# Token operands of the stationary side laid out in turns, read with a step of two elements

## The chip, the cores and the metric

The kernel runs on one core of one Trainium2 chip. The metric is the device time of one launch in microseconds. The profile shows TensorE as two rows: PE for the matmuls and PEld for the loads of their stationary operand.

## What is computed

The reference is an encoder trunk of two layers over 256 tokens of width 2048. Cut to its frame, one layer is:

```python
h = rms_norm(x, ln1_g[l])
proj = h @ w_in[l]                       # 2048 -> 4608 columns: q, k, v of two head groups
...                                      # QK norm, rotary, two kinds of windowed attention -> oa, ob
o = jnp.concatenate([rms_norm(oa, on_a[l]), rms_norm(ob, on_b[l])], axis=-1)
x = x + o @ w_out[l]                     # 2048 -> 2048
h2 = rms_norm(x, ln2_g[l])
u = depthwise_conv(h2 @ w_up[l], conv_w[l], conv_b[l])   # 2048 -> 2 x 5632, three taps over tokens
gate, up = u[..., :D_FF], u[..., D_FF:]
x = x + (jax.nn.silu(gate) * up) @ w_down[l]             # 5632 -> 2048
```

Everything is float32.

## The kernel before

**Numbers.** Every float32 operand of a large product is split in two float32r parts, a high one (ScalarE copies it with rounding) and a low one (VectorE subtracts the high part from the original). A product is then three matmuls: high by high, low by high and high by low. A tile of split tokens has the shape 128 x 2 x 256: partitions hold 128 of the features, then come the two parts, then the 256 tokens.

**Which side is stationary.** In the input projection (`q_win`), the output projection (`q_wout`), and the down-projection (`q_seven`, `q_plain`, `q_down`) 128 tokens are the stationary operand (a tile of 128 x 128) and 512 columns of weights move. In the up-projection (`q_up`) it is the other way: 128 columns of weights are stationary, and the tokens move, 512 columns for both parts or 256 for the high part alone. `q_seven` computes most of the down-projection by Strassen-like products: it takes sums and differences of token halves (`sums_mid`), which are split as the tokens are, and of weight blocks (`sums_first`, `sums_second`).

**The two halves.** The 256 tokens are two halves of 128, since a stationary operand has 128 columns. Before the change, half 0 stands in elements 0 to 127 of a part and half 1 in 128 to 255, so a stationary operand is 128 elements in a row. The tile names that the profile uses: `xs` are the split tokens of the two norms, `mid` (and, where the feed-forward needs more of them, `qT` and `qtok`) the split outputs of attention `os`, of the gate `gs` and of the sums `ss`; `whi` and `wlo` are the high and low parts of weights (some of them in `kT`, `v_a` and `v_b`). In a matmul's row the moving tile stands first after the arrow and the stationary one second: `mm<-whi,xs` has weights moving over stationary tokens, `mm<-xs,whi` tokens moving over stationary weights.

**Where the split tokens are written.** `prep_x` writes `xs` (argument `which` is 0 for the norm ahead of the input projection, 1 for the one ahead of the up-projection), `values` writes `os`, `high` and `low` in `glu` write `gs` out of `ms`, and `high` and `low` in `sums_mid` write the sums. Each of these is one instruction of 256 elements on ScalarE for the high part and one on VectorE for the low part. `ms`, the sums in `tq` and the PSUM tiles that they read keep their order of tokens.

**Order of work.** Weights come by DMA in tiles of 128 x 1024 (`raw`), in the order of a list of quanta, and are split some steps ahead of their matmuls (`split_w`, `high_w`, `low_w_dve`); part of the low parts are made by a DMA that adds (`low_w`). From the second of the feed-forward's 44 column blocks on, a class `Plan` sets the order on PE, ScalarE, VectorE and GpSimd by a table of due times and durations; elsewhere the framework's scheduler does. Some tile sizes are padded (1024 + 64 elements, `UP_AT`, `SHIFT`) so that tiles start at chosen addresses.

Of the kernel before, what the change touches and what calls it, by code (L numbers as in the profile page):

```python
# [11 lines left out]
F32 = mybir.dt.float32  # L12
F32R = mybir.dt.float32r
I32 = mybir.dt.int32
AF = mybir.ActivationFunctionType
# [3 lines left out]
P = 128  # L19
L = 2  # L20
T = 256
# [105 lines left out]
def encoder_kernel(  # L127
# [5 lines left out]
    nc = tc.nc  # L133
# [19 lines left out]
    ln_g = head[:, 0:2 * L * KD].rearrange("p (w l k) -> p w l k", w=2, l=L)  # L153
# [10 lines left out]
    def mm(ps, lhsT, rhs, start, stop):  # L164
        nc.tensor.matmul(ps, lhsT, rhs, start=start, stop=stop, skip_group_check=True)  # L165

    def rsqrt(ps, inv_n, dst, tag):
# [5 lines left out]
            e = e.rearrange("p (t h) -> p t h", t=TT)  # L173
        nc.gpsimd.tensor_tensor(dst, v, e, op=ALU.pow)

    def split(hi, lo, src, scale=None):

        if scale is None:
            high = nc.scalar.activation(hi, src, AF.Copy)  # L179
            nc.vector.tensor_sub(lo, src, hi.bitcast(F32))  # L180
        else:
            high = nc.scalar.activation(hi, src, AF.Copy, scale=scale)  # L182
            nc.vector.scalar_tensor_tensor(lo, src, scale, hi.bitcast(F32),
                                           op0=ALU.mult, op1=ALU.subtract)
        return high
# [11 lines left out]
    xs = {}  # L197
    st = {}

    def prep_x(l, which, k, src):  # L200

        xs[k] = act.tile([P, 2, T], F32R, name=f"xs{k}")
        split(xs[k][:, 0], xs[k][:, 1], src, ln_g[:, which, l, k:k + 1])

    def square_x(nb):
        if nb == 0:
# [117 lines left out]
    os = {}  # L324
# [147 lines left out]
    def values(l, grp, h):  # L472
        t = sm.pop(("T", grp, h))
        ps = psum.tile([P, T], F32, name="pv", bufs=1)
        if grp == "a":
            v, c = V["a", h // 4], (h % 4) * HD
            mm(ps[:, 0:KW], v[:, 0, c:c + HD], t[:, 0, 0:KW], True, False)
            mm(ps[:, T - KW:T], v[:, 1, c:c + HD], t[:, 1, 0:KW], False, True)
        else:
            v, c = V["b", 0], (h // 4) * HD  # L480
            for kt in range(TT):
                thrice(ps, [v[:, i, kt, c:c + HD] for i in range(2)], [w[:, kt, :] for w in t], kt == 0, kt == TT - 1)
        g = 0 if grp == "a" else 1
        if h == 0:
            acc_o[grp] = act.tile([P, T], F32, name=f"acc_{grp}")
        k = g * NH + h
        os[k] = act.tile([P, 2, T], F32R, name="mid", bufs=MIDS)
        split(os[k][:, 0], os[k][:, 1], ps, par["on_g"][:, l, g, h:h + 1])
        add_square(acc_o[grp], ps, h == 0)


# [11 lines left out]
    def three(ps, terms, hv, lv, first, last, apart=False):  # L503

        n = len(terms)
        order = [(x_part, w, tt) for x_part, w in ((0, hv), (1, hv), (0, lv)) for tt in range(TT)]
        if apart:
            order.sort(key=lambda o: o[2])
        for x_part, w, tt in order:
            for i, x2 in enumerate(terms):  # L510
                mm(ps[:, tt], x2[:, x_part, tt * P:(tt + 1) * P], w[:, i],
                   first and w is hv and x_part == 0 and i == 0, last and w is lv and i == n - 1)

    cur = {}
# [89 lines left out]
    gs = {}  # L604
# [35 lines left out]
    def glu(l, f, q, ps):  # L640
        ux = halo[f % 2]
        r = T // GRID_W
        e = ends.get((l, f), 0.0)
        own = {}
        taps = [[par["conv"][:, l, i, j * NF + f:j * NF + f + 1] for i in range(4)] for j in range(2)]
        k = lambda n, g=f: (n, l, g)

        def read(part):
            own[part] = work.tile([P, 2, T], F32, name="prob", bufs=2)
            with tc.high_priority(offset=4 * AHEAD_PRIO):  # L650
                nc.scalar.activation(own[part], ps[:, :, part], AF.Copy)  # L651

        def scale():
            nc.vector.tensor_mul(ux[:, :, r:r + T], own[0], st["r2"][:, None, :].to_broadcast([P, 2, T]))

        def sides():
            nc.scalar.activation(ux[:, :, 1:r], ux[:, :, T:T + r - 1], AF.Copy)
            nc.scalar.activation(ux[:, :, T + r:T + 2 * r - 1], ux[:, :, r + 1:2 * r], AF.Copy)

        def tap(name, j, o, i):  # L660
            if name not in own:
                own[name] = work.tile([P, 2, T], F32, name="pT", bufs=4)
            src = ux[:, j, o:o + T]
            if name == "y":
                nc.scalar.activation(own["y"][:, j], src, AF.Identity, scale=taps[j][i], bias=taps[j][3])  # L665
            else:
                nc.scalar.activation(own[name][:, j], src, AF.Copy, scale=taps[j][i])  # L667

        def gate():
            m = ms[f] = work.tile([P, T], F32, name="bias", bufs=2)  # L670
            nc.vector.tensor_mul(m, own[0][:, 0, :], own["y"][:, 1, :])

        def high():
            gs[f] = middle(l, f)
            nc.scalar.activation(gs[f][:, 0], ms[f], AF.Copy)

        def low():
            nc.vector.tensor_sub(gs[f][:, 1], ms[f], gs[f][:, 0].bitcast(F32))

        plan.act(k("t"), 512, e + 2.5, lambda: read(0), [("pe", q, 1), k("gate", f - 1)])  # L680
        plan.act(k("t2"), 512, e + 3.0, lambda: read(1), [k("t"), k("sum", f - 1)])
        plan.dve(k("sum"), 512, e + 5.0, lambda: nc.vector.tensor_add(own[0], own[0], own[1]), [k("t"), k("t2")])
        plan.dve(k("scale"), 512, e + 6.0, scale, [k("sum")] + [k(n + str(j), f - 2) for n in "yab" for j in range(2)])
        plan.op(k("sides"), "ACT", 0.3, e + 7.0, sides, [k("scale")])
        for n, o, i, dep, old in (("y", r, 1, "scale", k("add_b", f - 1)), ("a", 0, 0, "sides", k("gate", f - 1)),
                                  ("b", 2 * r, 2, "sides", k("add_a", f - 1))):
            for j in range(2):
                plan.act(k(n + str(j)), T, e + 7.5 + i % 3 + 0.5 * j, lambda n=n, j=j, o=o, i=i: tap(n, j, o, i),
                         [k(dep), old], 2 if n == "y" else 1)
        for n in "ab":  # L690
            plan.dve(k("add_" + n), 512, e + (11.0 if n == "a" else 12.0),
                     lambda n=n: nc.vector.tensor_add(own["y"], own["y"], own[n]),  # L692
                     [k("y0"), k("y1"), k(n + "0"), k(n + "1")])
        plan.act(k("silu"), T, e + 13.0, lambda: nc.scalar.activation(own[0][:, 0, :], own["y"][:, 0, :], AF.Silu),
                 [k("add_a"), k("add_b")])
        old = [("vsum", l, f // 2 - 1), k("low", f - 2)]
        plan.dve(k("gate"), T, e + 14.0, gate, [k("silu")] + old)
        plan.act(k("high"), T, e + 18.0, high, [k("gate")], when=lambda: sum(free.values()) > 0)
        plan.dve(k("low"), T, e + 24.0, low, [k("high")])
        if f % 2 and f < NF - CHUNKS[-1] + PART:  # L700
            sums_mid(l, f // 2)
# [3 lines left out]
    def sums_mid(l, p):  # L705
# [11 lines left out]
            nc.vector.tensor_sub(v[:, 2], m1[:, a], m1[:, b])  # L717
            nc.vector.tensor_sub(v[:, 3], m2[:, a], v[:, 1])

        part = lambda i: own["v"][:, 2 * i:2 * i + 2].rearrange("p j n -> p (j n)")  # L720

        def high(i):
            own[i] = middle(l, 2 * p)
            nc.scalar.activation(own[i][:, 0], part(i), AF.Copy)

        def low(i):
            t = own[i]
            nc.vector.tensor_sub(t[:, 1], part(i), t[:, 0].bitcast(F32))
            for j in range(2):
                ss[p, 2 * i + j] = t[:, :, j * P:(j + 1) * P]  # L730

        reads = [("low", l, 2 * p), ("low", l, 2 * p + 1)]
        plan.dve(k("vsum"), P, e + 24.0, sums, reads + [("vlow1", l, p - 2)], 4)
# [5 lines left out]
    def q_seven(l, c, m, i):  # L739

        f = sum(CHUNKS[:c]) + 2 * i
        p = f // 2
        a, b = slice(0, P), slice(P, T)

        def body(q, part, hi, lo):
            if i == 0 and part == 0:
                t = psum.tile([P, 2, 512], F32, name="mm", bufs=2)
                ps = {1: t[:, 0], 6: t[:, 1]}
                for n, name, k in ((5, "S", 2), (7, "S", 2), (3, "tr", 1), (4, "pv", 1)):
# [1 line left out]
                cur["seven"] = ps  # L751
            ps = cur["seven"]
            hv, lv = (w.rearrange("p (k n) -> p k n", k=2) for w in (hi, lo))
            todo = (((1, gs[f][:, :, a], 1), (3, ss[p, 3], 0)),
                    ((7, ss[p, 2], 0), (5, ss[p, 0], 1)),
                    ((4, gs[f + 1][:, :, b], 0), (6, ss[p, 1], 1)))[part]
            for n, x2, j in todo:
                for x_part, w in ((0, hv), (1, hv), (0, lv)):
                    mm(ps[n], x2[:, x_part], w[:, j], i == 0 and x_part == 0 and w is hv,
# [65 lines left out]
    def q_plain(l, c, m):  # L825

        f0 = sum(CHUNKS[:c])

        def body(q, half, hi, lo):
            ps = cur["seven"][1]  # L830
            hv, lv = (w.rearrange("p (k n) -> p k n", k=2) for w in (hi, lo))
            for x_part, w in ((0, hv), (1, hv), (0, lv)):
                for i in range(2):
                    mm(ps, gs[f0 + 4 * half + 2 * i + 1][:, x_part, 0:P], w[:, i],
                       False, half == 1 and i == 1 and w is lv)
            if half == 1 and m == 1:
                for i in range(PAIRS):
                    drop(l, f0 // 2 + i, (1,))
        return body
# [495 lines left out]
```

## Time and profile before

| | |
|---|---|
| time, median of 3 runs | 2070.07 us (2069.88 to 2070.23) |
| the profiled execution's own time | 2070.64 us |
| its span | 2068.9 us |
| PE busy | 2062.4 us, 10720 matmuls |
| PEld busy | 1769.9 us, 10720 loads |
| VectorE (DVE) busy | 1706.1 us |
| ScalarE (ACT) busy | 1549.3 us |
| GpSimd (POOL) busy | 157.6 us |
| HBM | 412.80 MB read, 201 GB/s over the span |

The span runs from the first to the last instruction on the core. The end of a matmul is modelled in the profile and reaches into the next one, so that the time of a stream of matmuls is read from one start to the next. Stretches, from the start of the span: input projection, attention and output projection up to about 339 us (second layer: from about 1020 to 1369 us), and the feed-forward after each.

### The profile page before, as it was taken

The page shows a single profiled execution, that of the slowest core. Times are in us where ns is not written, and L with a number is a line of the kernel's source. Part 1 is how long each engine was busy: PE and PEld are TensorE (multiplying, and loading weights), DVE is VectorE, ACT ScalarE, POOL GpSimd, SP SyncE. Part 2 cuts the span into 40 slices and gives each one's busy share as a digit, 9 for nine tenths or more (in the row PEclk, how much of TensorE's full clock was granted, in tenths as well). Part 3 has the DMA queues.
Part 4 walks back from the last instruction along what each step waited for, and adds up shares of the span by engine and source line. Part 5 has one row for each costly group of instructions (what it writes and reads, how often), then busy time and mean ns, then how long its engine had stood idle before and what let it go on. Part 6 is the DMA issues. An engine that isn't in the chain of part 4 may idle for free.

```text
span 2068.9 us, 30510 instructions
## 1 busy us (share of the span) xinstructions
PE 2062.4 (100%) x10720; PEld 1769.9 (86%) x10720; DVE 1706.1 (82%) x2576; ACT 1549.3 (75%) x2595; POOL 157.6 (8%) x170
## 2 busy tenths in 40 slices
PE   9999999999999999999999999999999999999999
PEld 8888888888888888888888888888888888888887
DVE  7786655889999999999757866558899999999995
ACT  7566646988888888888555665479888888888883
POOL 0011000000000000000000111000000000000000
PEclk9999999999999999999999999999999999999999
DMA  9655557888888888898655555678788888888883
GB/s 350 204 163 163 171 180 200 256 233 249 256 265 251 257 251 259 250 263 255 219 181 177 173 166 164 191 211 242 239 251 258 254 256 264 256 252 259 253 261 131
DMA packets 134009, 472.48 MB, mean 228 GB/s; under 512 B 15328, under 2 KB 17888, under 8 KB 133856
## 3 DMA queue, kind: packets, MB, share of 16 engines
q1 hardware_dynamic: 117872, 413.87, 61.2%
q0 software_dynamic: 15264, 55.58, 15.0%
q8 instruction: 84, 1.38, 0.3%
q10 hardware_dynamic: 720, 1.08, 0.2%
q14 instruction: 69, 0.57, 0.1%
HBM read 412.80 MB, written 2.10 MB: 201 GB/s over the span
## 4 chain that ended last, share of the span: by engine, by line
PE 99%; DMA 0%; ACT 0%; ACTq 0%; DVE 0%; issue 0%
PE mm L165 85%; PE S L165 6%; PE pv L165 4%; PE tr L165 3%; PE tr L460 1%; PE tr L381 1%; PE S L220 1%; DMA mid<-in_xT 0%; ACT v_a L335 0%; ACT whi L1002 0%; ACT mid L182 0%; ACT xs L182 0%; DVE x L872 0%; ACTq L1105 0%; ACTq L1098 0%
## 5 line engine op out<-in xcount | busy, mean ns | idle before, releaser
L165 PE MATMUL mm<-xs,whi 128*128 128x512 f32 x2320 | 810.0, 390 | 0.0
L1011 DVE TENSOR_TENSOR wlo<-raw,whi 128x1024 fp32r<-128x1024 f32 x503 | 613.0, 1220 | 185.0 <-ACT whi L1002 162.4
L1002 ACT ACTIVATE whi<-raw 128x1024 fp32r<-128x1024 f32 x569 | 596.2, 1055 | 222.2 <-PE mm L165 182.8
L165 PE MATMUL mm<-xs,wlo 128*128 128x256 f32 x2112 | 596.2, 282 | 0.0
L165 PEld LDWEIGHTS mm<-xs,whi 128*128 128x128 f32 x2320 | 435.3, 188 | 92.1 <-ACT prob L651 0.6
L165 PEld LDWEIGHTS mm<-xs,wlo 128*128 128x128 f32 x2112 | 399.0, 189 | 3.7
L165 PE MATMUL mm<-whi,xs 128*128 128x512 f32 x1152 | 294.8, 393 | 0.8 <-ACT whi L179 0.7
L165 PE MATMUL mm<-whi,mid 128*128 128x512 f32 x928 | 255.2, 393 | 0.4 <-ACT v_a L335 0.4
L165 PEld LDWEIGHTS mm<-whi,xs 128*128 128x128 f32 x1152 | 212.7, 188 | 43.5 <-ACT whi L179 1.3
L165 PEld LDWEIGHTS mm<-whi,mid 128*128 128x128 f32 x928 | 169.9, 188 | 34.3 <-ACT v_a L335 0.9
L165 PE MATMUL mm<-xs,kT 128*128 128x512 f32 x496 | 174.6, 390 | 0.0
L165 PE MATMUL mm<-wlo,xs 128*128 128x512 f32 x576 | 158.7, 392 | 0.0
L667 ACT ACTIVATE pT<-halo,conv 128x256 f32<-128x256 f32 x352 | 157.8, 498 | 0.0
L165 PE MATMUL mm<-wlo,mid 128*128 128x512 f32 x486 | 152.7, 393 | 0.0
L651 ACT ACTIVATE prob<-mm 128x512 f32<-128x512 f32 x176 | 103.6, 591 | 50.2 <-PE mm L165 49.8
L692 DVE TENSOR_TENSOR pT<-pT 128x512 f32<-128x512 f32 x176 | 120.8, 686 | 10.7 <-ACT pT L665 4.3
L165 PEld LDWEIGHTS mm<-wlo,xs 128*128 128x128 f32 x576 | 107.1, 188 | 21.5
L165 PEld LDWEIGHTS mm<-xs,kT 128*128 128x128 f32 x496 | 93.1, 188 | 19.5
L165 PEld LDWEIGHTS mm<-wlo,mid 128*128 128x128 f32 x486 | 90.9, 188 | 19.1
L665 ACT ACTIVATE pT<-halo,conv 128x256 f32<-128x256 f32 x176 | 103.7, 590 | 0.0
L165 PE MATMUL mm<-xs,v_a 128*128 128x256 f32 x352 | 99.3, 282 | 0.0
L165 PE MATMUL mm<-xs,v_b 128*128 128x256 f32 x352 | 99.3, 282 | 0.0
(251 smaller groups left out, 3043.1 us busy)
## 6 DMA issues: line engine op xcount, KB each, us to landing
raw<-in_w_up SPq DMA_DIRECT2D x262, 512.0 KB, 5.6
raw<-in_w_in SPq DMA_DIRECT2D x142, 512.0 KB, 4.4
raw<-in_w_seven SPq DMA_DIRECT2D x110, 512.0 KB, 5.9
raw<-in_w_out SPq DMA_DIRECT2D x64, 512.0 KB, 3.8
tabs<-in_w_up SPq DMA_DIRECT2D x48, 512.0 KB, 5.7
aux<-in_w_up SPq DMA_DIRECT2D x42, 512.0 KB, 5.5
v_a<-raw POOLq DMA_DIRECT2D x39, 512.0 KB, 6.5
v_b<-raw POOLq DMA_DIRECT2D x39, 512.0 KB, 6.5
```

What stands on the lines that cost most here:

```text
L165: nc.tensor.matmul(ps, lhsT, rhs, start=start, stop=stop, skip_group_check=True)
L220: nc.tensor.transpose(ps[:, j, tt * P:(tt + 1) * P], x[:, tt, (k + j) * P:(k + j + 1) * P], ident)
L381: nc.tensor.transpose(ps[:, j, tt * P:(tt + 1) * P], qn[tt][:, p + j, :], ident)
L460: nc.tensor.transpose(ps[:, kt, tt * P:(tt + 1) * P], p[:, tt, kt * P:(kt + 1) * P], ident)
L651: nc.scalar.activation(own[part], ps[:, :, part], AF.Copy)
L665: nc.scalar.activation(own["y"][:, j], src, AF.Identity, scale=taps[j][i], bias=taps[j][3])
L667: nc.scalar.activation(own[name][:, j], src, AF.Copy, scale=taps[j][i])
L692: lambda n=n: nc.vector.tensor_add(own["y"], own["y"], own[n]),
L1002: highs[s] = nc.scalar.activation(his[s], source(s), AF.Copy)
L1011: nc.vector.tensor_sub(los[s], source(s), his[s].bitcast(F32))
```

## The change

Wherever split tokens become stationary, the two halves stand in turns: token n of half h is at element 2n + h of its part. The writers of `xs` (with `which` 0), `os`, `gs` and the sums write through a view with a step of two, and the matmuls read half h through a view with a step of two that begins at element h. The `xs` of the up-projection, which move, are left as they were, and so are all weights. The same matmuls are issued with the same numbers.

```diff
+    def halves_of(t):
+        return t.rearrange("p c (n h) -> p c h n", h=2)
+
+    def in_turns(t):
+        return t.rearrange("p (n h) -> p h n", h=2)
+
+    def in_line(t):
+        return t.rearrange("p (h n) -> p h n", h=2)
...
         xs[k] = act.tile([P, 2, T], F32R, name=f"xs{k}")
-        split(xs[k][:, 0], xs[k][:, 1], src, ln_g[:, which, l, k:k + 1])
+        hi, lo = xs[k][:, 0], xs[k][:, 1]
+        if which == 0:
+            hi, lo, src = in_turns(hi), in_turns(lo), in_line(src)
+        split(hi, lo, src, ln_g[:, which, l, k:k + 1])
...
-        split(os[k][:, 0], os[k][:, 1], ps, par["on_g"][:, l, g, h:h + 1])
+        split(in_turns(os[k][:, 0]), in_turns(os[k][:, 1]), in_line(ps), par["on_g"][:, l, g, h:h + 1])
...
-                mm(ps[:, tt], x2[:, x_part, tt * P:(tt + 1) * P], w[:, i],
+                mm(ps[:, tt], halves_of(x2)[:, x_part, tt], w[:, i],
...
-            nc.scalar.activation(gs[f][:, 0], ms[f], AF.Copy)
+            nc.scalar.activation(in_turns(gs[f][:, 0]), in_line(ms[f]), AF.Copy)
...
-            nc.vector.tensor_sub(gs[f][:, 1], ms[f], gs[f][:, 0].bitcast(F32))
+            nc.vector.tensor_sub(in_turns(gs[f][:, 1]), in_line(ms[f]), in_turns(gs[f][:, 0].bitcast(F32)))
...
-        part = lambda i: own["v"][:, 2 * i:2 * i + 2].rearrange("p j n -> p (j n)")
+        part = lambda i: own["v"][:, 2 * i:2 * i + 2]
...
-            nc.scalar.activation(own[i][:, 0], part(i), AF.Copy)
+            nc.scalar.activation(in_turns(own[i][:, 0]), part(i), AF.Copy)
...
-            nc.vector.tensor_sub(t[:, 1], part(i), t[:, 0].bitcast(F32))
+            nc.vector.tensor_sub(in_turns(t[:, 1]), part(i), in_turns(t[:, 0].bitcast(F32)))
             for j in range(2):
-                ss[p, 2 * i + j] = t[:, :, j * P:(j + 1) * P]
+                ss[p, 2 * i + j] = halves_of(t)[:, :, j]
...
-            todo = (((1, gs[f][:, :, a], 1), (3, ss[p, 3], 0)),
+            todo = (((1, halves_of(gs[f])[:, :, 0], 1), (3, ss[p, 3], 0)),
                     ((7, ss[p, 2], 0), (5, ss[p, 0], 1)),
-                    ((4, gs[f + 1][:, :, b], 0), (6, ss[p, 1], 1)))[part]
+                    ((4, halves_of(gs[f + 1])[:, :, 1], 0), (6, ss[p, 1], 1)))[part]
...
-                    mm(ps, gs[f0 + 4 * half + 2 * i + 1][:, x_part, 0:P], w[:, i],
+                    mm(ps, halves_of(gs[f0 + 4 * half + 2 * i + 1])[:, x_part, 0], w[:, i],
```

More of the change, by code (lines that the diff above doesn't have):

```diff
@@ L742, in q_seven @@
         p = f // 2
-        a, b = slice(0, P), slice(P, T)
         def body(q, part, hi, lo):
```

## The prediction

> **What bounds the kernel now.** I read the page first (busy times, the clock row, the chain), then the chain in order of time, the timeline of single matmuls, the groups by form, and the waits of PE.
>
> ```profile
> span 2068.9 us, 30510 instructions
> PE 2062.4 (100%) x10720; PEld 1769.9 (86%) x10720; DVE 1706.1 (82%) x2576; ACT 1549.3 (75%) x2595; POOL 157.6 (8%) x170
> PEclk9999999999999999999999999999999999999999
> PE 99%; DMA 0%; ACT 0%; ACTq 0%; DVE 0%; issue 0%
> ...
> PE pv L165 <- DVE halfpi L161: 1.1, 1, 1.1
> PE mm L165 <- ACT whi L179: 0.7, 1, 0.7
> PE mm L165 <- ACT v_a L335: 0.4, 2, 0.2
> ```
>
> The matmuls are the path from end to end, at an undisturbed clock, and what PE waited for others comes to 2.2 us. So time is won or lost only in the distance from the start of one matmul to the next. The chain in order of time gives that distance.
>
> ```profile
> 10.30 65.60 PE mm L165 x288
> 76.34 16.15 PE mm L165 x71
> 338.70 81.25 PE mm L165 x468
> ```
>
> Each piece runs up to where the next begins, so a matmul of the input projection takes 65.60 / 288 = 227.8 ns, or 16.15 / 71 = 227.5 ns. All of these have tokens stationary and 512 moving columns. The third piece is the up-projection, whose matmuls of 512 and 256 columns alternate with weights stationary: 173.6 ns on average, 347 a pair. It is not changed.
>
> Is 227.5 ns all arithmetic? Two plain fp32 shapes give a yardstick.
>
> ```profile
> L165 PE MATMUL S<-kT,qT 128*128 128x160 f32 x64 | 10.8, 302 | 0.0
> L220 PE MATMUL S<-ident,x 128*128 128x128 f32 x96 | 14.0, 272 | 0.0
> ...
> 204.96 1.25 PE L165 MATMUL S<-kT,qT 128*128 128x160 f32 x8
> 1026.37 1.03 PE L220 MATMUL S<-ident,x 128*128 128x128 f32 x8
> ...
> 661.98 0.39 PE L165 MATMUL mm<-xs,whi 128*128 128x512 f32 x1
> 662.21 0.28 PE L165 MATMUL mm<-xs,wlo 128*128 128x256 f32 x1
> 662.33 0.39 PE L165 MATMUL mm<-xs,whi 128*128 128x512 f32 x1
> ```
>
> Eight of 160 columns: (1250 - 302) / 7 = 135.4 ns each; eight of 128: (1030 - 272) / 7 = 108.3. The difference is 0.85 ns a column, with 0 to 2 ns left over per instruction. The kernel's other matmuls (fp32r) need 230 ns for 512 columns and 120 for 256, so 110 / 256 = 0.43 a column, half of that. At 0.42 ns, 512 columns are 215 ns, and with 1 ns fixed 216. About 11.5 ns of every 227.5 are then something else, although the fp32 rows load a stationary operand per instruction too. What is special to the fp32r ones is that they take a moving column in half the time.
>
> ```profile
> 1007.55 0.39 PE L165 MATMUL mm<-whi,mid 128*128 128x512 f32 x1
> 1007.55 0.19 PEld L165 LDWEIGHTS mm<-whi,qT 128*128 128x128 f32 x1
> 1007.77 0.39 PE L165 MATMUL mm<-whi,qT 128*128 128x512 f32 x1
> 1007.78 0.19 PEld L165 LDWEIGHTS mm<-whi,mid 128*128 128x128 f32 x1
> ...
> 660.61 1.07 PE L165 MATMUL mm<-whi,mid 128*128 128x512 f32 x4
> 661.51 0.63 PE L165 MATMUL mm<-v_a,mid 128*128 128x512 f32 x2
> ```
>
> Each weight load begins with the matmul before its own, and so reads SBUF while that one streams. And the addresses matter: four matmuls from 660.61 take 0.90 us (225 ns each), the two from 661.51 up to 661.98 take 235 each. Those two differ in the tile v_a: in the built program all other token matmuls have both operands at the same address modulo 256 bytes, there the moving one lies 32 bytes lower. I read the 11.5 ns as collisions of the two reads.
>
> **The change, part by part.** In the built programs each engine has the same instructions in the same order and every tile its old address; only access patterns differ.
>
> (a) Stationary reads. 4392 fp32r matmuls read tokens with a step of two: by the loops 1728 in the input projection, 768 in the output projection, 1296 in q_seven, 216 in q_plain, 384 in q_down. The first is checked by two rows below (1152 + 576).
>
> ```profile
> L165 PE MATMUL mm<-whi,xs 128*128 128x512 f32 x1152 | 294.8, 393 | 0.8 <-ACT whi L179 0.7
> L165 PE MATMUL mm<-wlo,xs 128*128 128x512 f32 x576 | 158.7, 392 | 0.0
> L165 PEld LDWEIGHTS mm<-whi,xs 128*128 128x128 f32 x1152 | 212.7, 188 | 43.5 <-ACT whi L179 1.3
> ```
>
> No row has a stepped stationary read, so its price is bounded. How fast does the load advance? The 256-column matmul at 662.21 is followed after 120 ns, and the load that it covers began with it: 128 columns in at most 120 ns, about 0.9 ns a column, or 4 bytes per 0.9 ns. The fp32r moving operand advances 4 bytes per 0.42 ns, twice as fast, so its reads run over the load's again and again. The fp32 moving operand advances 4 bytes per 0.85 ns, level with the load, and there nothing is lost. With a step of two the load advances 8 bytes per 0.9 ns, level with the fp32r moving operand: a fixed distance, as in the fp32 rows. Best end: 11.5 ns of each of the 4392 go, -50.5 us. Worst end: each stationary operand spans 1024 bytes instead of 512, and if the loss is paid per piece of SBUF touched it doubles, +50.5 us. I take the gain, since the fp32 rows are the nearest case of two reads at one speed; -48 us, a little being kept for the first matmuls after each interruption.
>
> [...]
>
> (b) The load itself. It needs up to 120 of 216 ns; at one and a half times it stays hidden (180), at twice (240) it would set the distance: +12.5 ns on 4392, +55 us. I take it hidden.
>
> (c) Stepped writes. 232 splits of 256 elements on ACT and as many on DVE (32 xs, 32 os, 88 gs, 80 sums) write with a step of two, and DVE reads the high part so.
>
> ```profile
> L678 DVE TENSOR_TENSOR mid<-bias,mid 128x256 fp32r<-128x256 f32 x74 | 30.9, 418 | 0.0
> L1011 DVE TENSOR_TENSOR wlo<-raw,whi 128x1024 fp32r<-128x1024 f32 x503 | 613.0, 1220 | 185.0 <-ACT whi L1002 162.4 <-PE mm L165 17.5 <-ACT mid L182 4.2
> L675 ACT ACTIVATE mid<-bias 128x256 fp32r<-128x256 f32 x74 | 30.4, 410 | 6.5 <-DVE bias L671 5.1
> L1002 ACT ACTIVATE whi<-raw 128x1024 fp32r<-128x1024 f32 x569 | 596.2, 1055 | 222.2 <-PE mm L165 182.8 <-issue 23.9 <-DVE raw L964 9.6
> ...
> 345.00:1020.00 675.00, 675.00 (x3617) 585.35 (x3616) 613.96 (x875) 566.52 (x941) 45.86 (x54) 1.00 0.85 249
> 1700.00:2050.00 350.00, 350.00 (x1850) 302.63 (x1849) 321.73 (x444) 285.97 (x462) 21.70 (x25) 1.00 0.84 249
> ```
>
> The slopes are (1220 - 418) / 768 = 1.04 ns an element on DVE and 0.84 on ACT. Bounds: nothing, or a doubled slope, +0.27 us and +0.21 us each. The two window rows (their columns are length, PE, PEld, DVE, ACT, POOL) are the feed-forward of a layer and its tightest half. Some 84 splits a layer stand there: doubled they add 22 us to DVE against 61 us of idle time in the first, about 11 us against 28 us in the second. So the cover is DVE's idle time; it is gone at 3.5 times the slope. Then the low weight parts, which stand behind the splits in DVE's queue, come late to PE. Outside it the splits are on the path only where PE has nothing else: kernel start and ends of attention, about eight places, up to 0.5 us each. I take +1 us.
>
> [...] No row here shows a stepped write.
>
> (d) Other queues. No DMA, semaphore or wait is added. With PE faster, input-projection weights are wanted about 5% sooner; the DMA share there is in this row.
>
> ```profile
> 0.00:345.00 345.00, 342.91 (x1679) 288.44 (x1680) 238.94 (x445) 209.24 (x363) 35.31 (x38) 1.00 0.65 206
> ```
>
> At 0.65 of the engines, and DVE busy 239 of 345 us, there is room: nothing.
>
> Sum: the profiled execution took 2070.64 us, 1.7 more than its span. 2070.6 - 48 + 1 = 2023.6; it stands 0.6 over the median of the runs shown, so 2023.
>
> **Rivals.**
> 1. *Twice the pieces* (other side, slower). The loss is paid per piece of SBUF that the load touches, so it doubles, at the same place in the same 4392 matmuls: 2070 + 50 + 1 = 2121. For it: 11.5 ns is a steady toll and hardly depends on what else runs. Against: the fp32 matmuls load the same operand and pay 0 to 2 ns. It decides as soon as the distance grows beyond 227.5 ns.
> 2. *No effect* (the change doesn't do what it says). The toll is fixed for an fp32r weight load, and only the 235 ns of v_a were a collision: 2070 to 2072. For it: 227.5 and 227.8 in different stretches, and 347 - 0.42 x 768 = 24 ns a pair, 12 each, with other addresses in the up-projection. [...]
> 3. *The load becomes the bound*, as in (b): 2125 at twice its time, far more beyond.
> 4. *DVE becomes the bound*, from 3.5 times the slope on: 2023 plus some 10 us for each 0.5 times more.
>
> **How the numbers follow.** Chances: forecast 0.60 (own range 2012, which is all the toll and 1.7 ns more, to 2059, a quarter of what I take); no effect 0.13; twice the pieces 0.20; the load as bound 0.05; DVE as bound in earnest 0.02. The first two hold 0.73, so the range must reach into the slower cases: 2012 to 2124 holds forecast, no effect and most of rival 1. About 0.2% (4 us) is what a measurement of this kernel can tell from no change. Faster by more than that 0.60, within it 0.13, slower 0.27.
>
> **What would show it.** Right: token matmuls of the input projection 214 to 220 ns apart, those of v_a changed otherwise than the rest, the up-projection still 347 ns a pair; weight loads still about 188 ns long. ACT's and DVE's splits at 410 to 700 ns, without new waits of PE. Wrong: a distance of 227 (rival 2), near 239 with loads of old length (rival 1), loads well over 188 ns (rival 3), or PE waiting for wlo in the feed-forward (rival 4).

## The result, and the profile after

The changed kernel took 2095.29 us (median of 4 runs, 2095.03 to 2095.45) against 2070.15 us: 1.0120 times the time, with a 95% interval of 1.0103 to 1.0138. It was forecast faster, at 2023 us; it is slower by 25 us.

The page of the kernel after, its header and the share of the chain by engine:

```profile
span 2093.5 us, 30506 instructions
...
PE 2087.7 (100%) x10720; PEld 1796.5 (86%) x10720; DVE 1707.6 (82%) x2576; ACT 1555.6 (74%) x2595; POOL 157.5 (8%) x170
...
PEclk9999999999999999999999999999999999999999
...
PE 99%; DMA 0%; ACT 0%; SPq 0%; DVE 0%; issue 0%; ACTq 0%
```

PE is still the path from end to end, at the same granted clock (1.0 in both profiled executions). The chain in order of time (start, length, piece) shows where the time went:

```profile
10.35 67.47 PE mm L165 x288
78.26 16.73 PE mm L165 x71
345.66 81.26 PE mm L165 x468
```

The 71 matmuls of the second piece took 16.15 us and now take 16.73, that is 227.5 and 235.6 ns each; the 288 of the first went from 227.8 to 234.3. The up-projection, unchanged by the edit, has its 81.25 us again, give or take 10 ns. In the trace, the distances from each of the 4392 token matmuls to the next start add up to 1008.3 us before and 1032.9 us after. The difference of 24.6 us is that of the spans (2093.5 - 2068.9).

Groups by form of the kernel after, with the weight load and the splits (busy, mean ns):

```profile
L165 PEld LDWEIGHTS mm<-whi,xs 128*128 128x128 f32 x1152 | 219.9, 194 | 41.9 <-ACT whi L1013 0.6
L687 ACT ACTIVATE mid<-bias 128x256 fp32r<-128x256 f32 x74 | 32.0, 433 | 8.2 <-DVE bias L683 7.3
L690 DVE TENSOR_TENSOR mid<-bias,mid 128x256 fp32r<-128x256 f32 x74 | 31.0, 419 | 0.0
```

A load with a step of two takes 194 ns in place of 188, still less than the 233.7 ns from one matmul to the next. The stepped writes cost 23 ns on ScalarE (410 to 433) and 1 ns on VectorE (418 to 419). The waits of PE in the kernel after are those of before, 1.7 us in all (2.2 before):

```profile
PE pv L165 <- DVE halfpi L161: 1.1, 1, 1.1
PE mm L165 <- ACT v_a L347: 0.4, 2, 0.2
PE mm L165 <- ACT whi L1013: 0.2, 1, 0.2
```

### The profile page after: what moved, and what is told of

It reads as the page before. It is cut to its first block, busy times and chain, and to the rows that moved or that the text cites. A ratio compares the mean times of both kernels' runs of the same rounds, so it can differ in the third digit from the quotient of the medians.

```text
span 2093.5 us, 30506 instructions
## 1 busy us (share of the span) xinstructions
PE 2087.7 (100%) x10720; PEld 1796.5 (86%) x10720; DVE 1707.6 (82%) x2576; ACT 1555.6 (74%) x2595; POOL 157.5 (8%) x170
## 4 chain that ended last, share of the span: by engine, by line
PE 99%; DMA 0%; ACT 0%; SPq 0%; DVE 0%; issue 0%; ACTq 0%
PE mm L165 85%; PE S L165 6%; PE pv L165 4%; PE tr L165 3%; PE tr L472 1%; PE S L232 1%; PE tr L393 1%; DMA raw<-in_w_in 0%; ACT v_a L347 0%; SPq L946 0%; ACT whi L1013 0%; ACT mid L191 0%; DVE x L883 0%; ACTq L1013 0%
## 5 line engine op out<-in xcount | busy, mean ns | idle before, releaser
L165 PE MATMUL mm<-whi,xs 128*128 128x512 f32 x1152 | 301.0, 397 | 0.2 <-ACT whi L1013 0.2
L165 PE MATMUL mm<-whi,mid 128*128 128x512 f32 x928 | 260.1, 397 | 0.4 <-ACT v_a L347 0.4
L165 PEld LDWEIGHTS mm<-whi,xs 128*128 128x128 f32 x1152 | 219.9, 194 | 41.9 <-ACT whi L1013 0.6
L165 PEld LDWEIGHTS mm<-whi,mid 128*128 128x128 f32 x928 | 175.0, 194 | 34.3 <-ACT v_a L347 0.9
```

## The experiments

All of them alter only access patterns or addresses of the token matmuls and their splits. "Distance" below is the mean from start to start, in the trace, over token matmuls that have three others on each side; before it is 227.2 ns, after 233.7. The piece of 71 matmuls of the input projection is the row to compare: 16.15 us before, 16.73 after. In the kernel after it is one of the slower pieces, with 235.6 ns a matmul where most streams have 233.3. A stream is a run of token matmuls without another matmul between them.

**Reads or writes?** The first kernel steps only the reads, the second only the writes.

```diff
 # e1: the kernel before, with
-mm(ps[:, tt], x2[:, x_part, tt * P:(tt + 1) * P], w[:, i],
+mm(ps[:, tt], x2.rearrange("p c (n h) -> p c h n", h=2)[:, x_part, tt], w[:, i],
 # e2: the kernel after, with
-mm(ps[:, tt], halves_of(x2)[:, x_part, tt], w[:, i],
+mm(ps[:, tt], x2[:, x_part, tt * P:(tt + 1) * P], w[:, i],
 # both: the same in q_seven, q_plain and for the sums
```

> The kernel before, with nothing changed but the stationary reads: the token matmuls read with a step of two, while the splits still write the tokens in a row (so each half takes every second token, and tokens are mixed). Three theories of the 227.5 ns that became 233. Theory A, pieces: a weight load takes time from the streaming matmul for each piece of SBUF that it touches; all of the loss is then in the reads: 233 ns between starts, 2094 to 2096 us. Theory B, timing: the loss depends on how the load's addresses run against the moving ones; same time here. Theory W, the stepped writes or what waits for them cost it: 2070 us here.

> The changed kernel with its stepped writes, but the matmuls read 128 elements in a row as before (tokens are mixed). Theories A and B: 227.5 ns between starts, 2070 to 2072 us. Theory W: 2095 us.

The chain of the kernel with stepped reads alone:

```profile
78.12 16.73 PE mm L165 x71
```

And of the one with stepped writes alone:

```profile
76.10 16.15 PE mm L165 x71
```

Reads alone: 2095.05 us, ratio 1.0119 (1.0104 to 1.0134). Writes alone: 2070.23 us, ratio 0.9999 (0.9989 to 1.0008). The whole loss is in the stationary reads; the stepped writes, which took ScalarE 433 ns in place of 410 in the kernel after, cost no time.

**Does it go by what the load touches?** Steps of four and of zero:

```diff
+# e3
+t.rearrange("p c n -> p (c n)").rearrange("p (n q) -> p q n", q=4)[:, 2 * h + c]
+# e4
+t[:, c, P * h:P * h + 1].to_broadcast([P, P])
```

> Reads alone, with a step of four elements over both parts of the tile (parts and tokens are mixed). Theory A with the toll growing with the memory that the load spans: 6 ns came with the second 512 bytes, so 2048 bytes cost 18 ns over the row-wise read: 245.5 ns, 2070 + 4392 x 0.018 = 2149 us. Theory A with pieces of 8 bytes (64 of them in a row, 128 from a step of two on): no more than with a step of two, 233 ns, 2095 us. Theory B, lock-step: the load runs twice as fast as the moving operand, as far from its speed as the row-wise read: near 227 ns, 2070 us.

> Reads alone, with a step of zero: all 128 stationary columns are the first token of the half (the product is not the reference's). [...] Theory B: a load that stands still is passed by the moving operand again and again: no less than 227 ns. A fixed toll for each load: 227.5 ns, 2070 us.

The chain with a step of four:

```profile
78.92 16.81 PE mm L165 x71
```

Its weight loads, by form:

```profile
L165 PEld LDWEIGHTS mm<-whi,xs 128*128 128x128 f32 x1152 | 284.8, 311 | 0.6 <-ACT whi L1005 0.3 <-ACT whi L182 0.2
```

The chain with a step of zero:

```profile
77.72 16.45 PE mm L165 x71
```

Step four: 2124.44 us, ratio 1.0261 (1.0241 to 1.0282), but a distance of only 235.1 ns in the stream, and not 245.5; no expectation had named that time. Its loads take 311 ns, and that shows where a stream starts anew: in the piece of 71, the distance from the first token matmul after four transposes to the second was 314 ns and is 438. Of the 54 us, 31 are inside the streams (some 4000 distances, 7.7 ns each) and 23 in the first distances of the 193 streams, 120 ns each. Step zero: 2083.48 us, ratio 1.0063 (1.0043 to 1.0083), 231.0 ns. A load that reads one word 128 times leaves the stream at 231.0 ns, one that reads a row of 512 bytes at 227.2. A toll by pieces, which was rival 1's reason, would have fallen with a single word, however large a piece is; it is refuted. A toll fixed for each load, 227.5 ns, is refuted too.

The loads themselves (mean busy time, `mm<-whi,xs`) took 188 ns in a row and at a step of zero, 194 at a step of two and 311 at a step of four.

**Offset and direction.** The weights that move are shifted by 32 bytes in both kernels, and then read from the last column to the first.

```diff
 # e5 (kernel before), e6 (kernel after)
-o = UP_AT if kind_of(s) == "up" else 0
+o = UP_AT if kind_of(s) == "up" else 8
 # e7 (kernel before), e8 (reads of step two, as e1); the same in q_seven and q_plain
-... w[:, i],
+... w[:, i, ::-1],
```

> The kernel before with the split weights that move over stationary tokens 32 bytes further on (nothing else changes). The runs so far: reads alone make the whole loss; with a step of zero the distance is 231 ns, with one 227.2, with two 233.6, with four 235.1, so it doesn't go by the pieces that the load touches. Theory B2, settling: what a load takes depends on the phase in which its reads fall against the moving ones, that phase carries over from matmul to matmul, and each address pattern settles on its own value (227 = 34 x 6.67 ns, 233.3 = 35 x 6.67 ns); an offset of 32 bytes then settles elsewhere: 233 ns, as the moving v_a of before, 2070 + 4392 x 0.006 = 2094 to 2097 us. Theory A2, a toll for each load that only its step sets: 227.5 ns, 2070 us.

> The changed kernel with the same shift by 32 bytes of the weights that move. Theory B2: another value than 233.6 ns, most likely on the steps of 6.67 ns: 226.7 ns (2068 to 2071 us) if the offset suits the step of two, or 233 to 240 ns (2095 to 2123 us) if not. Theory A2: 233.6 ns, 2095 us.

> The kernel before with the moving weights read from the last of the 512 columns to the first in the token matmuls (the columns of these products come out in reversed order). Theory B2, in which it matters how the two address streams run against each other: another value than 227.2 ns, in either direction, between 216 and 240 (2020 to 2125 us). Theory A2, or a toll that only goes by the phase in time: 227 ns, 2070 us.

> Reads with a step of two (splits in a row, tokens mixed) and the moving columns reversed as well. If the two streams at equal speed ran against each other in the changed kernel, they now run side by side at a fixed distance, or the other way round. Theory lock-step: 216 to 218 ns, 2070 - 4392 x 0.010 = 2022 to 2030 us. Theory B2 without lock-step: between 227 and 240 ns, 2070 to 2125 us. Theory A2: 233.6 ns, 2095 us.

The chain of the kernel before with the shift:

```profile
78.24 16.57 PE mm L165 x71
```

And with a step of two and the moving columns reversed:

```profile
78.20 16.58 PE mm L165 x71
```

| kernel | distance, ns | time, us | ratio (95%) |
|---|---|---|---|
| e5, in a row, shift 32 | 233.5 | 2094.50 | 1.0115 (1.0086 to 1.0144) |
| e6, step 2, shift 32 | 233.8 | 2096.40 | 1.0124 (1.0095 to 1.0154) |
| e7, in a row, moving reversed | 233.4 | 2096.10 | 1.0123 (1.0093 to 1.0152) |
| e8, step 2, moving reversed | 235.3 | 2103.67 | 1.0159 (1.0130 to 1.0189) |

The kernel before loses the same 6 ns by a shift of 32 bytes, without any step. And where the prediction took both reads to run at equal speed, the matmuls stand 233.7 ns apart in one direction and 235.3 in the other; neither comes near 216. Lock-step has fallen. e6 came out at the lower edge of the second of its two expectations (233 to 240 ns).

**Is the toll a clash at all, and how rare is 227?** The moving operand stands still; and three more offsets.

```diff
 # e9 (kernel before); the same in q_seven and q_plain
-... w[:, i],
+... w[:, i, 0:1].to_broadcast([P, 512]),
 # e10: shift 16 elements; e11: 4; e12 (kernel after): 16
```

> The kernel before with the moving operand of the token matmuls read with a step of zero: 512 times the same column of weights (those products are not the reference's); the stationary reads are in a row as before. Theory C1: what a load takes is a clash of two streams of addresses in SBUF; a moving operand that stands still no longer runs through memory, and the distance falls towards the 216 ns of the yardstick, 2070 - 4392 x 0.011 = 2020 to 2030 us. Theory C2: it doesn't need the moving addresses at all (the load's or the array's own doing, or the sharing of a port by time): 227 to 235 ns, 2070 to 2105 us.

> The kernel before with the weights that move over tokens 64 bytes further on. In the settled streams of before, after and the reversed read all distances are multiples of 6.67 ns, in which the moving operand advances 64 bytes. If that is the period of the address pattern, 64 bytes change nothing: 227 ns, 2069 to 2072 us. If the place within a longer pattern counts, or the offset of zero is a case of its own: 233 ns, 2095 us.

> The kernel before with the weights that move over tokens 16 bytes further on. With the settling theory each offset has its own value: 227 ns would mean that several offsets are as good (2070 us), 231 to 236 ns that the offset of before is a rare one (2085 to 2105 us), and under 225 ns (under 2062 us) that there is a better one. A toll that only the step sets: 2070 us.

> The changed kernel with the weights that move over tokens 64 bytes further on. With a pattern that repeats every 64 bytes: 233.6 ns, 2095 us, as without the shift. Otherwise 227 to 240 ns, 2068 to 2123 us.

The chain with a moving operand that stands still:

```profile
72.87 15.33 PE mm L165 x71
```

And its timeline, eight matmuls and the start of the next group:

```profile
80.48 1.89 PE L165 MATMUL mm<-whi,xs 128*128 128x512 f32 x8
82.21 1.03 PE L165 MATMUL mm<-wlo,xs 128*128 128x512 f32 x4
```

The same stretch of the kernel before, from which e9 is made:

```profile
81.67 1.98 PE L165 MATMUL mm<-whi,xs 128*128 128x512 f32 x8
83.48 1.07 PE L165 MATMUL mm<-wlo,xs 128*128 128x512 f32 x4
```

Still: 1.73 us for eight, 216 ns each; before: 1.81 us, 226 each. The still operand makes 2027.28 us (0.9791, 0.9763 to 0.9820): with as many columns, loads and bytes of stationary operand the toll is gone. So the toll came only with a moving operand that runs through memory (227.2 ns against 216), and the prediction's yardstick of 216 ns was right. That it is a clash with the load's reads is shown for the 6 ns that come with the load's step alone (e1). For the 10.7 ns of before it is argued, since every matmul here has a load. What speaks for it: in the trace of before, the up-projection's next start comes 228.6 ns after a matmul of 512 columns and 118.6 after one of 256; with the prediction's 0.42 ns a column and 1 ns fixed, an estimated 12.6 and 10.1 ns of these are toll, so half the columns under a whole load don't pay half the toll. The offsets: e10 229.2 ns and 2078.48 us (1.0040, 1.0024 to 1.0056), e11 231.7 ns and 2087.76 us (1.0084, 1.0054 to 1.0113), e12 233.4 ns and 2095.11 us (1.0119, 1.0090 to 1.0148). A pattern that repeats every 64 bytes would have left e10 at 227.2, so that expectation missed. Of all patterns tried in which every column is a new word, the one of before has the shortest distance.

**Equal speed or half demand?** The prediction had taken lock-step from fp32 matmuls, whose moving operand needs twice the time per column (the prediction's 0.85 ns against 0.43). The last runs make the fp32r operand as slow, by taking each of 256 columns twice, once with the load level with it (by the prediction's estimate of 0.9 ns a column) and once not; and put the still operand beside a load of step two.

```diff
 # e13: the kernel before; e14: with reads of step two, as e1
-... w[:, i],
+... w[:, i, 0:256, None].to_broadcast([P, 256, 2]),
 # e15: e9 with reads of step two, as e1
```

> The kernel before, with each of 256 moving columns taken twice in a row in the token matmuls (512 columns, the second half of the weights' columns unused; those products are not the reference's). The moving operand then runs through memory at half speed, level with a load that reads in a row, as in the fp32 rows from which the prediction took its lock-step. Lock-step: 216 ns, 2027 us. Theory D, slack (a moving operand at full rate wants the memory all the time and loses what the load takes; at half the rate it has room): 216 ns too, so this run counts together with the next. If neither holds: 227 to 235 ns, 2070 to 2105 us.

> The same with stationary reads of step two (tokens mixed), so that the load again runs through memory twice as fast as the moving operand. Lock-step: the loss is back, 227 to 235 ns, 2070 to 2105 us. Theory D: 216 ns as in the run before, 2027 us.

> The moving operand with a step of zero as in the run that gave 216 ns, and stationary reads of step two (tokens mixed; products not the reference's). If the load at a step of two costs something of its own, apart from the clash: over 216 ns, at most 222 (2053 us). If all of the 6 ns are clash: 216 ns, 2027 us.

The chain with columns taken twice and loads in a row:

```profile
73.10 15.33 PE mm L165 x71
```

With columns taken twice and loads of step two:

```profile
73.19 15.34 PE mm L165 x71
```

e13: 216.4 ns, 2025.30 us (0.9782, 0.9753 to 0.9810). e14: 216.0 ns, 2022.40 us (0.9768, 0.9739 to 0.9796). e15: 216.3 ns, 2023.26 us (0.9772, 0.9744 to 0.9800). When a new word comes only with every second column nothing over the 216 ns is lost, with the load in a row (e13) or at a step of two (e14): lock-step is out, and theory D, slack at half the rate, fits. Its reason, that the memory is then read less, isn't shown; a repeated word on the load's side saved nothing (e4, 231.0 ns). And a load of step two costs the stream nothing of its own (e15, 216.3 ns); its 6 ns appear only beside a moving operand that takes a new word for every column (e1), and in that sense are clash.

No pattern tried computes the reference faster than the kernel before does.

## Why the prediction was wrong, point by point

- **What bounds the kernel.** Right: PE's distances, and nothing else. The 11.5 ns over the yardstick of 216 ns are real and go when the moving operand stands still, as e9 shows. The timeline that stood for the role of addresses was read from starts rounded to 10 ns: from start to start the two matmuls of `v_a` take 234 and 231 ns, those ahead of them 226 to 227, and the pairs of `v_b`, which the built program places 32 bytes lower too, take as much. The contrast is there, with 6 ns in place of 10.
- **(a), the step that failed.** "With a step of two the load advances ... level with the fp32r moving operand: a fixed distance, as in the fp32 rows." The fp32 rows differ from the fp32r ones in two things, the ratio of speeds and the rate at which the moving operand takes new words. The prediction credited the first; e13 and e14 show that it is the second. A moving operand that takes a new word for every column at full rate lost 11 to 19 ns per matmul here, with load steps from zero to four; one at half the rate lost none (216.4 and 216.0 ns with steps of one and two). The level speeds were themselves an estimate: the prediction took the load at 0.9 ns a column from the 120 ns between two starts, while its rows of loads have 188 ns for 128 columns, 1.5 ns each. Which of the two is the pace of its reads, no run shows. The term was -48 us and came out +24.6 us: 4392 matmuls, about 5.6 ns each.
- **What the step did.** The toll is 10.7 ns in a row (226.7 less 216), 17.3 at a step of two (233.3), 15 at zero and 19 at four. In trace order, a stream of before goes 235, 233, 236, 224, 231, 236, 228, 233, 231 ns after the transposes ahead of the piece of 71, enters the same row further on or skips it after the other interruptions, and then stays at 226 to 227 until its last matmul. The kernel after stays at 233 to 234 in most streams; in a few it alternates between 229 and 238, and in some, the piece of 71 among them, it repeats 235, 238, 233. So equal matmuls in one stream don't pay equal tolls (distances of 224 to 236 ns before, 233 to 239 in the piece of 71 after), and how far apart they stay changed with the step (226.7 and 233.3 ns) and with the offset (a mean of 233.5 ns in e5). That the matmul ahead sets a toll is an inference from these rows. The change left the case that settles lowest of those tried. Why a stream settles where it does isn't known; 226.7 and 233.3 ns are 34 and 35 times 6.67, but the 235.6 ns of the piece of 71 are no such multiple, and e5, e10 and e11 don't settle on one value (e10 repeats 226, 229, 232).
- **Rival 2.** No effect, at 0.13, fell. With fp32r at full rate the load's reads count: e1 changes them alone, and 227.2 ns become 233.6. Where a new word comes with every second column they don't: 216.4 ns in a row and 216.0 at a step of two (e13 and e14).
- **(b).** Right: the load, 194 ns, stays hidden inside the streams. Where one starts anew, the distance of 314 ns ahead of the piece's second matmul became 326 in the kernel after, and 438 at a step of four (e3).
- **(c).** Right in kind, and +1 us was too much: e2 shows none. The doubled slope that bounded it (+0.21 us on ScalarE) came out at 0.02 us.
- **(d).** Right: PE's waits didn't grow.
- **Rivals and range.** Rival 1 had the side but not the reason, and twice the size: 239 ns and 2121 us expected, 233.7 ns and 2095 us measured, and pieces refuted by e4. The clash was priced as all or nothing, gone or doubled; a middle value had no case of its own. Chances of 0.60 for faster rested on one inference from rows that differed in two things. That 2095 us lies within 2012 to 2124 is luck: the range had been stretched towards rival 1, and no case in it gave that time. Of the signs, one came true beside the wrong mechanism: the pairs of `v_a` did change otherwise than the rest, from 234 and 231 ns to 233 and 239.

## What to carry to other kernels

When two rows differ in two things, a mechanism that explains the difference by one of them is a guess until a kernel alters that one alone; the cheapest such kernel here was a broadcast moving operand, which reads one word in place of 512 without changing the size of the matmul. In this kernel the steps, offsets and directions of the two operands were worth 2 to 8 ns in 227 per matmul, and every edit to them that kept a new word for every column lost 0.4 to 1.6 per cent or, with a load of step four, 2.6. Judge such an edit by the distance from start to start in one undisturbed stream.

## What was not expected of the hardware

- A load that reads a single word 128 times leaves the stream at 231.0 ns, between 227.2 for 128 words in a row and 233.7 for every second word, so its toll isn't a matter of bytes.
- The toll isn't the same for equal matmuls in a row: after an interruption the distances go through up to nine values before they settle at 226 to 227 ns (before), or stay in a cycle of three to the stream's end (235, 238, 233 ns in the piece of 71 of the kernel after).
- A load of step four takes 311 ns, longer than the 235 ns between matmuls, and yet the stream runs at 235: only the first distance of a stream shows it, 438 ns in place of 314.
- Writing every second word cost VectorE 1 ns in 418 and ScalarE 23 ns in 410.
